# A hybrid decoder layer in fp32: Strassen products without the short step in one more chunk, and a tile of its own for the rows that scale x

## The chip, the cores and the metric

One core of one Trainium2 chip runs the whole layer. The metric is the device time of one execution in microseconds, the median of several runs. The profile is of one further execution of the same program.

## The reference, cut to what matters

256 tokens of width 2048, one layer, all in fp32. Between the parts stands a layer norm with gain g and offset b.

```
x <- LN0(alpha*x + 0.5*SwiGLU_1(x))
z  = x @ W_in                      (nine projections)
m  = sigmoid(gate_conv)*(yA @ Wa) + sigmoid(gate_hgrn)*(yB @ Wb)
x <- LN1(alpha*x + m @ W_out)
x <- LN2(alpha*x + 0.5*SwiGLU_2(x))
x <- LN3(alpha*x + sigmoid(x @ W_pg) * (p @ W_pp))

def swiglu(x, w_in, w_out):
    a, u = jnp.split(x @ w_in, 2, axis=-1)
    return (jax.nn.silu(a) * u) @ w_out
```

The hidden width of each SwiGLU is 5504, so w_in is 2048 x 11008 and w_out 5504 x 2048.

## The kernel before, in words

**Products.** The tokens are two tiles of 128 (t = 0, 1). Activations stand still in TensorE, weights stream past it, 512 columns at a time. For fp32 accuracy each product of a k-tile (128 rows of weights) is three passes (`passes`, L1035): high half of x with high half of the weights (L1039), high with low (L1040), low with high (L1041). The high half of a weight tile (`wh`) is a cast by ScalarE (L973), the low half (`wl`) a subtraction by VectorE (L984); raw weights come by DMA from the SP queue (L913) into a ring `raw` of 4 tiles of two k-tiles each, 512 KB. The operands of x are made the same way by `halves`: `xh` by ScalarE (L284), `xl` by VectorE (L285).

**Stages.** lead1, ffn1, tail1, hgrn, merge, lead2, ffn2, tail2, ple. A feed-forward stage cuts its hidden width into 11 chunks: ch 0 with 512 columns and ch 1 with 384 are plain products (`Unit`); ch 2 to 10 are `Quad`s, which do the two tiles of tokens and two halves of the k-tiles by Strassen's seven products for eight. ch 0 runs in the lead stage, the rest in ffn. Between chunks stand the products with w_out (`out_unit`) for the chunks before; these go in groups of two chunks and four columns of 512, two columns after each chunk. So two of them follow ch 2 and ch 3 each, of 7 k-tiles, and two follow ch 4 and ch 5 each, of 8.

**Short step.** A Quad multiplies 16 k-tiles: 8 in two full Strassen steps, and 8 that are left. With the argument `short` (L79) two of those 8 are multiplied by one more Strassen step of half the size (`short_step`: h1 to h4, with three additions of weights by VectorE at L952, called h2, h3 and h4; h2 is 1024 columns wide, the others 512), in the order `ORDER`; without it all 8 are plain products, in the order `ORDER8`. `ORDER8` has 60 products of a k-tile, `ORDER` 59. In before ch 2 is without the short step and ch 3 to 10 with it (L498).

**The end of a chunk.** When the seven banks of a Quad are done, five small functions combine them on VectorE (all recorded at L463) and ScalarE: `first` to `fifth`. `third` begins with `silu<-h,bank`, which needs the bank of product p6.

**Norms.** `layer_norm(t, i, scale, stat)` scales x by mean and deviation (L425), and makes the operands of the next stage with g and b folded in by ScalarE (L419). x itself, for the residual, still has to be multiplied by g and added to b: that is `affine_rows`, for each column of 512 and both tiles of tokens, deferred to a later tick (a tick is one step of some matmuls). It loads a row of g and a row of b, spread over 128 partitions (256 KB each), into a slot of the weights' ring (tile `gb`, L397), and four ticks later multiplies (L402) and adds (L403). For layer norm 1, the one ahead of lead2, column c's rows are loaded 10 + 7c ticks after the norm.

**Sums.** For the Strassen products the operands need sums of x's quarters (`sums`, called at ch 1, additions at L319) in the tiles `yT` and in one more tile `s` from the ring "11" of region `high`.

**What sets the order.** Each engine runs its instructions in the order in which a scheduler put them. `feed` issues loads, additions, casts and splits of weights as slots come free; `defer` and `tick` place the rest. A queue never passes an instruction that waits.

Of the kernel before, what the change touches and what calls it, by code (L numbers as in the profile page):

```python
# [10 lines left out]
F32 = mybir.dt.float32  # L11
# [6 lines left out]
P = 128  # L18
D = 2048
S = 256  # L20
NT = 2
DFF = 5504
CW = 1024
CC = 512
KG = 2
NRAW = 4
# [110 lines left out]
def hybrid_layer(ctx: ExitStack, tc: tile.TileContext, x, p, ln_g, ln_b, ffn1_w_in, ffn1_w_out, mix_w_in,  # L137
# [13 lines left out]
    rp = pool("rp", side="right")  # L151
    st = pool("st", side="right")
    region = {}
# [8 lines left out]
    def open_region(kind):  # L162


        if kind.startswith("tail"):
            region.pop("hctx").close()
        region["pool"] = reopen("ctx", kind, "left")
        region["kind"] = kind
        if kind.startswith("lead"):
            region["high"] = reopen("hctx", kind + "h", "right")  # L170
            held.update(dict.fromkeys(HIGH, 0), on=False)
        if kind.startswith("ffn"):
            roles = {"a": 7, "t": 1}
        else:
            roles = {"t": 2, "a": 4, "h": 2}
        free = deque(sorted(banks, key=lambda n: used_at[n]))
        for role, n in roles.items():
            role_of[role] = [free.popleft() for _ in range(n)]
# [22 lines left out]
    def defer(delay, fn):  # L201
        insort(later, (state["tick"] + delay, fn), key=lambda e: e[0])
# [37 lines left out]
    def settle(c):  # L240

        while c in unsettled:
            later.pop(0)[1]()
# [61 lines left out]
    plain = {}  # L305

    def high(part, name):

        return region["high"].tile([P, KG, CC], F32, tag="b" + part, name=name, bufs=HIGH[part])
# [5 lines left out]
        return plain[t, c // 2][:, c % 2, :]  # L315

    def sums(stat):
        def both(o, a, b, op):
            nc.vector.tensor_tensor(out=o, in0=a, in1=b, op=op)  # L319

        def four(x11, x12, x21, x22, s1, s2, s3, s4):
            both(s3, x11, x21, ALU.subtract)
            both(s1, x21, x22, ALU.subtract)
            both(s2, s1, x11, ALU.subtract)
            both(s4, x12, s2, ALU.add)

        lo, hi, spare = [plain[t, 0] for t in range(NT)], [plain[t, 1] for t in range(NT)], high("11", "s")
        x = [lo[0][:, 0, :], lo[0][:, 1, :], lo[1][:, 0, :], lo[1][:, 1, :]]
        s3 = spare[:, 0, :]

        def low_sums():
            four(*x, x[2], x[0], s3, x[1])

        def made(n, src):
            halves(stat, n, 0, src, 4, "s")


        short = spare[:, 1, :]

        def short_sums():  # L340
            y = [hi[t][:, 0, i * P : (i + 1) * P] for t in range(NT) for i in range(2)]
            four(*y, *(short[:, i * P : (i + 1) * P] for i in range(4)))

        def made_short():
            halves(stat, "short", 0, short, 4, "s")
            h, l = stat.parts["short", 0]
            for i in range(4):
                stat.parts[f"s{i + 1}", 1] = h[:, i : i + 1, :], l[:, i : i + 1, :]

        def delta(c):  # L350
            d = hi[0][:, c % 2, :]
            both(d, d, hi[1][:, c % 2, :], ALU.subtract)
            halves(stat, "d", c, d, 4, "s")

        todo = (low_sums, lambda: made("s1", x[2]), lambda: made("s2", x[0]), lambda: made("s3", s3),
                lambda: made("s4", x[1]), short_sums, made_short, lambda: delta(2), lambda: delta(3),
                lambda: held.update(on=True))
        for i, fn in enumerate(todo):
            defer(1 + 2 * i, fn)
# [30 lines left out]
        nc.vector.bn_aggr(mv, stats[t])  # L390
        return mv[:, 0:1], rsqrt_of(mv[:, 1:2], 1, 1.0, LN_EPS / scale ** 2)

    def affine_rows(i, c, ts):

        gb = rp.tile([P, KG, CC], F32, tag="raw", name="gb", bufs=NRAW)
        for a, src in enumerate((ln_g, ln_b)):
            nc.sync.dma_start(gb[:, a, :], src[0, i : i + 1, c * CC : (c + 1) * CC].broadcast_to([P, CC]))  # L397

        def apply():
            for t in ts:  # L400
                xc = xt[t][:, c * CC : (c + 1) * CC]
                nc.vector.tensor_tensor(out=xc, in0=xc, in1=gb[:, 0, :], op=ALU.mult)  # L402
                nc.vector.tensor_tensor(out=xc, in0=xc, in1=gb[:, 1, :], op=ALU.add)  # L403
            unsettled.remove(c)

        defer(4, apply)

    def layer_norm(t, i, scale, stat):

# [19 lines left out]
        if t == NT - 1:  # L429
            for c in range(4):  # L430
                unsettled.add(c)
                defer(10 + 7 * c if stat is x2 else 40 + 20 * c, lambda c=c: affine_rows(i, c, range(NT)))

    def layer_norm_out(t, gb):
        mean, r = moments(t, 1.0)
# [7 lines left out]
    units = []  # L443

    def ffn(name, xs, w_in, w_out, ln_i, nxt):
# [7 lines left out]
        def in_units(ch, g, ci):  # L453
            c0 = starts[ch]
            w = starts[ch + 1] - c0
            if ch > 1:
# [32 lines left out]
                def fifth(ps):  # L489
# [5 lines left out]

                after = deque([(("p1",), first), (("p3", "p5"), second), (("p6", "p7"), third),
                               (("p2",), fourth), (("p4",), fifth)])
                units.append(Quad(xs, w_in, (c0, DFF + c0), CC, after, ch > 2))  # L498
                return
            silu = {}  # L500

# [45 lines left out]
    x0, x1, x2, x3 = Stat(), Stat(), Stat(), Stat()  # L547
# [322 lines left out]
    for u in units:  # L870
# [17 lines left out]
        for blk in u.blocks:  # L888
            for ks in blk:
                i = len(plan)  # L890
# [118 lines left out]


    open_region(units[0][0])

    warm = ptile("a", "warm")
# [112 lines left out]
```

## Time and profile before

| | us |
|---|---|
| median of 3 runs | 2228.91 |
| lowest, highest | 2226.73, 2230.83 |
| profiled execution | 2225.66 |
| its span | 2223.9 |

The granted TensorE clock has a mean of 0.996 in that execution. Line numbers in the profile are those of the kernel before. PE is TensorE's matmuls, PEld its weight loads, DVE is VectorE, ACT is ScalarE, SP the queue that issues most DMAs. A matmul of 512 columns is shown as 0.39 us long, but successive ones overlap: the pace is read from their starts. In brackets behind a row of a timeline stands how long the engine was idle ahead of it and what ended that.

### The profile page before, as it was taken

How to read it: one execution, taken by the hardware profiler on the slowest of the kernel's cores; microseconds unless marked ns; L12 is line 12 of the kernel's file. 1: busy time of each engine (PE TensorE's matmuls, PEld its weight loads, DVE VectorE, ACT ScalarE, POOL GpSimd, SP SyncE). 2: the span in 40 equal slices, each digit the busy share in tenths (PEclk: the TensorE clock that was granted, in tenths of full speed). 3: DMA queues.
4: the chain of work that ended last, by engine and by line, in shares of the span. 5: the costliest groups of instructions: out<-in, count | busy, mean ns of one | idle time of the engine just before them, and what ended most of it. 6: DMA issues, size and time to landing. Idle time of an engine off the chain costs nothing.

```text
span 2223.9 us, 27084 instructions
## 1 busy us (share of the span) xinstructions
PE 2193.5 (99%) x10062; PEld 1827.2 (82%) x10062; DVE 1755.3 (79%) x2042; ACT 1156.0 (52%) x1357; POOL 9.9 (0%) x32
## 2 busy tenths in 40 slices
PE   9999999999999999999999999999999999999997
PEld 7987888888887888888888888788788888888886
DVE  6788999999985678567555875769899999999668
ACT  5555555555565434444444443645556555556463
POOL 1000000000000000000000000000000000000000
PEclk9999999999999999999999999999999999999998
DMA  7656666666663665555565665576566666665564
GB/s 252 222 185 198 210 205 189 191 207 208 199 202 113 203 193 171 181 161 152 189 194 184 206 193 191 181 231 189 182 199 206 201 211 198 202 202 188 173 216 156
DMA packets 225848, 430.00 MB, mean 193 GB/s; under 512 B 14252, under 2 KB 22964, under 8 KB 225716
## 3 DMA queue, kind: packets, MB, share of 16 engines
q1 hardware_dynamic: 225716, 428.27, 60.9%
q8 instruction: 79, 1.29, 0.2%
q14 instruction: 53, 0.43, 0.1%
HBM read 426.12 MB, written 2.10 MB: 193 GB/s over the span
## 4 chain that ended last, share of the span: by engine, by line
PE 92%; DVE 4%; DMA 2%; issue 1%; ACT 1%; SPq 0%; DVEq 0%; ACTq 0%
PE bank L1040 30%; PE bank L1041 30%; PE bank L1039 30%; PE bank L274 2%; DVE wl L984 2%; PE bank L636 1%; DMA gb<-in_ln_g_dram 1%; DVE raw L952 1%; ACT wh L973 0%; DMA gb<-in_ln_b_dram 0%; DMA raw<-in_ffn_w_in_dram 0%; DMA x<-in_x_dram 0%; DVE x L438 0%; DVE x L439 0%; ACT y L419 0%
## 5 line engine op out<-in xcount | busy, mean ns | idle before, releaser
L973 ACT CAST wh<-raw 128x1024 fp32r<-128x1024 f32 (+2 forms) x944 | 960.0, 1032 | 833.9 <-PE bank L1041 519.2
L984 DVE TENSOR_TENSOR wl<-raw,wh 128x1024 fp32r<-128x1024 f32 (+2 forms) x944 | 1113.6, 1200 | 283.1 <-ACT wh L973 262.0
L1040 PE MATMUL bank<-wl,xh 128*128 128x512 f32 (+1 forms) x1688 | 652.1, 387 | 1.2 <-DVE wl L984 1.0
L1041 PE MATMUL bank<-wh,xl 128*128 128x512 f32 (+1 forms) x1688 | 651.3, 387 | 1.5 <-DVE xl L285 1.5
L1039 PE MATMUL bank<-wh,xh 128*128 128x512 f32 (+1 forms) x1688 | 648.2, 388 | 1.7 <-ACT xh L284 1.6
L1039 PEld LDWEIGHTS bank<-wh,xh 128*128 128x128 f32 x1688 | 317.9, 188 | 62.9 <-ACT xh L284 2.6
L1040 PEld LDWEIGHTS bank<-wl,xh 128*128 128x128 f32 x1688 | 317.9, 188 | 62.7 <-DVE wl L984 2.8
L1041 PEld LDWEIGHTS bank<-wh,xl 128*128 128x128 f32 x1688 | 317.5, 188 | 62.6 <-DVE xl L285 2.2
L1040 PE MATMUL bank<-wl,gh 128*128 128x512 f32 x896 | 349.9, 391 | 4.3 <-DVE wl L984 4.1
L1041 PE MATMUL bank<-wh,gl 128*128 128x512 f32 x896 | 349.8, 392 | 0.0
L1039 PE MATMUL bank<-wh,gh 128*128 128x512 f32 x896 | 348.5, 393 | 0.0
L952 DVE TENSOR_TENSOR raw<-raw,raw 128x1024 f32<-128x1024 f32 (+1 forms) x176 | 206.3, 1172 | 6.2 <-DMA raw<-in_ffn_w_in_dram 4.5
L1040 PEld LDWEIGHTS bank<-wl,gh 128*128 128x128 f32 x896 | 168.7, 188 | 40.6 <-DVE wl L984 6.0
L1041 PEld LDWEIGHTS bank<-wh,gl 128*128 128x128 f32 x896 | 168.5, 188 | 34.5
L1039 PEld LDWEIGHTS bank<-wh,gh 128*128 128x128 f32 x896 | 168.3, 188 | 34.4 <-ACT pp L841 0.2
L1040 PE MATMUL bank<-wl,sh 128*128 128x512 f32 x464 | 180.6, 389 | 0.0
L1041 PE MATMUL bank<-wh,sl 128*128 128x512 f32 x464 | 180.5, 389 | 0.0
L1039 PE MATMUL bank<-wh,sh 128*128 128x512 f32 x464 | 179.2, 390 | 0.0
L1041 PEld LDWEIGHTS bank<-wh,sl 128*128 128x128 f32 x464 | 87.1, 188 | 18.2
L1039 PEld LDWEIGHTS bank<-wh,sh 128*128 128x128 f32 x464 | 87.1, 188 | 18.0
L1040 PEld LDWEIGHTS bank<-wl,sh 128*128 128x128 f32 x464 | 87.1, 188 | 18.0
L526 DVE TENSOR_TENSOR x<-x,bank 128x512 f32<-128x512 f32 x64 | 43.6, 681 | 21.6 <-PE bank L1041 21.5
(173 smaller groups left out, 1005.1 us busy)
## 6 DMA issues: line engine op xcount, KB each, us to landing
raw<-in_ffn_w_in_dram SPq DMA_DIRECT2D x288, 512.0 KB, 4.5
raw<-in_mix_w_in_dram SPq DMA_DIRECT2D x176, 512.0 KB, 4.7
raw<-in_ffn_w_out_dram SPq DMA_DIRECT2D x168, 512.0 KB, 4.7
raw<-in_ffn_w_in_dram SPq DMA_DIRECT2D x64, 256.0 KB, 3.0
raw<-in_mix_w_out_dram SPq DMA_DIRECT2D x32, 512.0 KB, 5.2
raw<-in_ple_w_gate_dram SPq DMA_DIRECT2D x32, 512.0 KB, 5.5
raw<-in_ffn_w_in_dram SPq DMA_DIRECT2D x32, 384.0 KB, 4.0
raw<-in_branch_w_conv_dram SPq DMA_DIRECT2D x16, 512.0 KB, 4.7
```

Source lines behind the costliest of these rows:

```text
L274: state["turned"] = nc.tensor.transpose(tp[:, i * P : (i + 1) * P], src[:, i * P : (i + 1) * P], ident).ins
L526: nc.vector.tensor_tensor(out=xc, in0=xc, in1=acc, op=ALU.add)
L636: nc.tensor.matmul(gp[:, (h * 2 + t) * 64 : (h * 2 + t + 1) * 64], kd[:, h, t * P : (t + 1) * P], qd[:, h, t, :], start=True, stop=True)
L952: nc.vector.tensor_tensor(out=out, in0=a, in1=b, op=ALU.add)
L973: nc.scalar.copy(h[:, :n, :w], raw[:, :n, :w])
L984: nc.vector.tensor_tensor(out=l[:, :n, :w], in0=raw[:, :n, :w], in1=h[:, :n, :w].bitcast(F32), op=ALU.subtract)
L1039: nc.tensor.matmul(acc, sh, wh[:, a, :n], start=first, stop=False)
L1040: nc.tensor.matmul(acc, sh, wl[:, a, :n], start=False, stop=False)
L1041: nc.tensor.matmul(acc, sl, wh[:, a, :n], start=False, stop=last)
```

## The change

It has two parts. First, `ch > 2` becomes `ch > 3`: ch 3 of both feed-forward stages is done without the short step, as ch 2 was. Second, the tile that `sums` used as `s` is now taken when a lead stage opens, under the name `spare`; in lead2 the rows of g and b for all four columns go by way of this one tile, and not by the weights' ring. Column c's rows are loaded 2 + 8c ticks after the norm and applied six ticks later. `sums` first finishes what is still to be scaled (`settle`). Layer norms 0 and 2 keep the ring and their ticks.

```diff
@@ open_region
             held.update(dict.fromkeys(HIGH, 0), on=False)
+            region["spare"] = high("11", "spare")
@@ sums
     def sums(stat):
+        for c in range(4):
+            settle(c)
+
@@ sums
-        lo, hi, spare = [plain[t, 0] for t in range(NT)], [plain[t, 1] for t in range(NT)], high("11", "s")
+        lo, hi, spare = [plain[t, 0] for t in range(NT)], [plain[t, 1] for t in range(NT)], region["spare"]
@@ affine_rows
-    def affine_rows(i, c, ts):
-
-        gb = rp.tile([P, KG, CC], F32, tag="raw", name="gb", bufs=NRAW)
+    def affine_rows(i, c, ts, gb, delay):
+
+        if gb is None:
+            gb = rp.tile([P, KG, CC], F32, tag="raw", name="gb", bufs=NRAW)
@@ affine_rows
-        defer(4, apply)
+        defer(delay, apply)
@@ layer_norm
-                defer(10 + 7 * c if stat is x2 else 40 + 20 * c, lambda c=c: affine_rows(i, c, range(NT)))
+                if stat is x2:
+                    defer(2 + 8 * c, lambda c=c: affine_rows(i, c, range(NT), region["spare"], 6))
+                else:
+                    defer(40 + 20 * c, lambda c=c: affine_rows(i, c, range(NT), None, 4))
@@ in_units
-                units.append(Quad(xs, w_in, (c0, DFF + c0), CC, after, ch > 2))
+                units.append(Quad(xs, w_in, (c0, DFF + c0), CC, after, ch > 3))
```

In the changed kernel the lines are a few further down: splits of weights are L992, additions of weights L960, steps at a chunk's end L471, the scaling L407 and L408, the loads of its rows L402, weights' DMAs L921, `xl` L286.

**VectorE at the end of ch 3 in before** (first feed-forward stage; `silu` and `h` are the tiles of the chunk's end, the addition of `raw_1838` is h2 of ch 4):

```order
L984 TENSOR_TENSOR wl<-raw_1539,wh 128x1024
L463 TENSOR_TENSOR silu<-silu,bank_83 128x512
L952 TENSOR_TENSOR raw_1362<-raw_1362,raw_1539 128x1024
L463 TENSOR_TENSOR silu<-h,bank_79 128x512
L984 TENSOR_TENSOR wl<-raw_1362,wh 128x1024
L463 TENSOR_TENSOR silu<-silu 128x512
L463 TENSOR_TENSOR h<-h,bank_81 128x512
L952 TENSOR_TENSOR raw_1838<-raw_1551,raw_1658 128x1024
L984 TENSOR_TENSOR wl<-raw,wh 128x1024 x2
```

**VectorE at the end of ch 4 in after** (the addition of `raw_2318` is h2 of ch 5):

```order
L992 TENSOR_TENSOR wl<-raw_2016,wh 128x1024
L471 TENSOR_TENSOR silu<-silu,bank_85 128x512
L960 TENSOR_TENSOR raw_1839<-raw_1839,raw_2016 128x1024
L471 TENSOR_TENSOR silu<-h,bank_82 128x512
L992 TENSOR_TENSOR wl<-raw_1839,wh 128x1024
L471 TENSOR_TENSOR silu<-silu 128x512
L471 TENSOR_TENSOR h<-h,bank_83 128x512
L960 TENSOR_TENSOR raw_2318<-raw_2028,raw_2135 128x1024
L992 TENSOR_TENSOR wl<-raw,wh 128x1024 x2
```

The same kinds of instructions stand in the same order, one chunk later; in after the end of ch 3 reads as that of ch 2 in before, with the addition for the next chunk ahead of `silu<-h,bank`.

**VectorE at the start of lead2 in before** (`x1_95` is the second tile of tokens, `mv`, `w` and `m` are its norm, `xl_11131` the first low operand of x2):

```order
L984 TENSOR_TENSOR wl_11013<-raw_10900,wh_11012 128x1024
L984 TENSOR_TENSOR wl_11077<-raw_10938,wh_11076 128x1024
L984 TENSOR_TENSOR wl_11083<-raw_10950,wh_11082 128x1024
L825 SCALAR_TENSOR_TENSOR x1_95<-x1_95,bank1_80 128x512
L984 TENSOR_TENSOR wl_11074<-raw_10912,wh_11073 128x1024
L367 BN_STATS bn_10618<-x1_95 128x6
L390 BN_AGGR mv_11050<-bn_10618 128x2
L375 TENSOR_SCALAR w_11052<-mv_11050 128x1
L377 TENSOR_SCALAR m_11053<-mv_11050 128x1
L984 TENSOR_TENSOR wl_11089<-raw_11016,wh_11088 128x1024
L285 TENSOR_TENSOR xl_11131<-yT_11121,xh_11130 128x512
```

**The same place in after** (`xl_11121` is the first low operand):

```order
L992 TENSOR_TENSOR wl_11058<-raw_10889,wh_11057 128x1024
L394 BN_AGGR mv_11033<-bn_10607 128x2
L992 TENSOR_TENSOR wl_11073<-raw_10939,wh_11072 128x1024
L379 TENSOR_SCALAR w_11035<-mv_11033 128x1
L381 TENSOR_SCALAR m_11036<-mv_11033 128x1
L407 TENSOR_TENSOR x0_94<-x0_94,spare_11056 128x512
L408 TENSOR_TENSOR x0_94<-x0_94,spare_11056 128x512
L992 TENSOR_TENSOR wl_11079<-raw_11064,wh_11078 128x1024
L992 TENSOR_TENSOR wl_11085<-raw_11070,wh_11084 128x1024
L286 TENSOR_TENSOR xl_11121<-yT_11111,xh_11120 128x512
```

Scaling of column 0 of the first tile of tokens and a split more now stand right ahead of the first low operand.

**SP's queue in lead2 in before** (`gb` are slots of the weights' ring):

```order
L913 DMA raw_11279<-in_ffn2_w_in_dram 128x2x512
L913 DMA raw_11291<-in_ffn2_w_in_dram 128x2x512
L397 DMA gb_11293<-in_ln_g_dram 128x512
L397 DMA gb_11293<-in_ln_b_dram 128x512
L913 DMA raw_11306<-in_ffn2_w_in_dram 128x2x384
L913 DMA raw_11318<-in_ffn2_w_in_dram 128x2x384
L913 DMA raw_11330<-in_ffn2_w_in_dram 128x2x384
L913 DMA raw_11360<-in_ffn2_w_in_dram 128x2x384
L397 DMA gb_11370<-in_ln_g_dram 128x512
L397 DMA gb_11370<-in_ln_b_dram 128x512
L913 DMA raw_11411<-in_ffn2_w_in_dram 128x2x384
```

**SP's queue in lead2 in after**, columns 1 to 3:

```order
L921 DMA raw_11109<-in_ffn2_w_in_dram 128x2x512
L402 DMA spare_11056<-in_ln_g_dram 128x512
L402 DMA spare_11056<-in_ln_b_dram 128x512
L402 DMA spare_11056<-in_ln_g_dram 128x512
L402 DMA spare_11056<-in_ln_b_dram 128x512
L402 DMA spare_11056<-in_ln_g_dram 128x512
L402 DMA spare_11056<-in_ln_b_dram 128x512
L921 DMA raw_11259<-in_ffn2_w_in_dram 128x2x512
```

The rows of g and b that had weights between them now follow one another, each into the same tile. On VectorE this stretch reads in after:

```order
L407 TENSOR_TENSOR x0_94<-x0_94,spare_11056 128x512
L407 TENSOR_TENSOR x1_95<-x1_95,spare_11056 128x512
L286 TENSOR_TENSOR xl_11191<-yT_11181,xh_11190 128x512
L408 TENSOR_TENSOR x0_94<-x0_94,spare_11056 128x512
L286 TENSOR_TENSOR xl_11209<-yT_11181,xh_11208 128x512
L408 TENSOR_TENSOR x1_95<-x1_95,spare_11056 128x512
L407 TENSOR_TENSOR x0_94<-x0_94,spare_11056 128x512
L407 TENSOR_TENSOR x1_95<-x1_95,spare_11056 128x512
L408 TENSOR_TENSOR x0_94<-x0_94,spare_11056 128x512
L408 TENSOR_TENSOR x1_95<-x1_95,spare_11056 128x512
L323 TENSOR_TENSOR yT_11150<-yT_11150,yT_11218 128x512
L286 TENSOR_TENSOR xl_11228<-yT_11218,xh_11227 128x512
```

Between the scalings of columns 1 and 2 (L407 multiplies, L408 adds) and the low operands there is no split of weights any more.

## Rows read from the trace of the kernel before

**Rows 1.** The page's busy time of each engine (share of the span, number of instructions), and the shares of the chain that ended last, by engine.
```profile
PE 2193.5 (99%) x10062; PEld 1827.2 (82%) x10062; DVE 1755.3 (79%) x2042; ACT 1156.0 (52%) x1357; POOL 9.9 (0%) x32
...
PE 92%; DVE 4%; DMA 2%; issue 1%; ACT 1%; SPq 0%; DVEq 0%; ACTq 0%
```

**Rows 2.** TensorE's waits over the whole span: which instruction, what it waited for: us in total, how often, the longest.
```profile
PE bank L1040 <- DVE wl L984: 5.1, 4, 2.0
...
PE bank L1039 <- ACT xh L284: 1.6, 2, 0.8
...
PE bank L1041 <- DVE xl L285: 1.5, 2, 0.8
PE bank L274 <- ACT pp L841: 1.5, 1, 1.5
PE bank L274 <- DVE gl L285: 1.0, 1, 1.0
```

**Rows 3.** TensorE's timeline at the end of ch 3 in the first feed-forward stage (two rows) and in the second: start, us, engine and line, operation, and in brackets the idle time ahead of it and what ended it.
```profile
192.50 0.40 PE L1041 MATMUL bank<-wh,xl 128*128 128x512 f32 x1
194.94 0.53 PE L1040 MATMUL bank<-wl,gh 128*128 128x512 f32 x1 [2.04 <-DVE wl L984]
...
1599.92 0.39 PE L1041 MATMUL bank<-wh,xl 128*128 128x512 f32 x1
1602.36 0.50 PE L1040 MATMUL bank<-wl,gh 128*128 128x512 f32 x1 [2.05 <-DVE wl L984]
```

**Rows 4.** TensorE's timeline around the change from the merge stage to lead2: the first and the last of 24 matmuls, the first two matmuls on x2's operands that waited, and the first use of a low operand of the third column of the second half.
```profile
1401.64 0.39 PE L1039 MATMUL bank<-wh,mh 128*128 128x512 f32 x1
...
1406.86 0.39 PE L1041 MATMUL bank<-wh,ml 128*128 128x512 f32 x1
...
1412.19 0.50 PE L1039 MATMUL bank<-wh,xh 128*128 128x512 f32 x1 [0.79 <-ACT xh L284]
...
1413.72 0.72 PE L1041 MATMUL bank<-wh,xl 128*128 128x512 f32 x1 [0.80 <-DVE xl L285]
...
1436.11 0.39 PE L1041 MATMUL bank<-wh,xl 128*128 128x512 f32 x1
```

**Rows 5.** Groups of VectorE's instructions by line and shape, from 145 to 190 us (chunks 2 and 3 of the first feed-forward stage): count, busy us, mean ns of one, idle us ahead of them.
```profile
L984 DVE TENSOR_TENSOR wl<-raw,wh 128x1024 fp32r<-128x1024 f32 x22 | 25.9, 1221 | 2.3 <-ACT wh L973 2.3
L952 DVE TENSOR_TENSOR raw<-raw,raw 128x1024 f32<-128x1024 f32 x8 | 9.8, 1221 | 0.1
...
L952 DVE TENSOR_TENSOR raw<-raw 128x512 f32<-128x512 f32 x1 | 0.7, 684 | 0.0
```

**Rows 6.** VectorE's timeline at the end of ch 3 of the first feed-forward stage.
```profile
189.59 0.69 DVE L463 TENSOR_TENSOR silu<-h,bank 128x512 f32<-128x512 f32 x1 [2.61 <-PE bank L1041]
190.19 1.22 DVE L984 TENSOR_TENSOR wl<-raw,wh 128x1024 fp32r<-128x1024 f32 x1
...
191.93 0.68 DVE L463 TENSOR_TENSOR h<-h,bank 128x512 f32<-128x512 f32 x1
192.53 1.22 DVE L952 TENSOR_TENSOR raw<-raw,raw 128x1024 f32<-128x1024 f32 x1
193.67 2.35 DVE L984 TENSOR_TENSOR wl<-raw,wh 128x1024 fp32r<-128x1024 f32 x2
```

**Rows 7.** Three stretches: length, busy time (and instructions) of PE, PEld, DVE, ACT and POOL, the granted TensorE clock as a share of full speed, the share of the DMA engines, GB/s.
```profile
195.20:198.70 3.50, 3.50 (x10) 2.71 (x10) 3.50 (x5) 0.00 (x0) 0.00 (x0) 0.51 0.65 221
1413.80:1417.30 3.50, 3.50 (x9) 2.76 (x10) 3.01 (x7) 3.50 (x10) 0.00 (x0) 0.51 0.86 281
1600.00:1610.00 10.00, 7.95 (x35) 6.30 (x34) 9.48 (x12) 2.73 (x3) 0.00 (x0) 1.00 0.77 236
```

**Rows 8.** VectorE's timeline at the start of lead2.
```profile
1405.57 3.49 DVE L984 TENSOR_TENSOR wl<-raw,wh 128x1024 fp32r<-128x1024 f32 x3
...
1412.99 0.68 DVE L285 TENSOR_TENSOR xl<-yT,xh 128x512 fp32r<-128x512 f32 x1
```

**Rows 9.** ScalarE's timeline at the same place.
```profile
1411.48 0.66 ACT L284 CAST xh<-yT 128x512 fp32r<-128x512 f32 x1
1412.78 1.05 ACT L973 CAST wh<-raw 128x1024 fp32r<-128x1024 f32 x1 [0.64 <-DMA raw<-in_ffn_w_in_dram]
```

**Rows 10.** The SP queue's timeline from 1406.5 to 1409 us: weights for lead2 (start, us until the last is issued, count).
```profile
1406.85 1.47 SPq L913 DMA_DIRECT2D raw<-in_ffn_w_in_dram  x2
```

**Rows 11.** Pieces of the chain of waits from 1430 to 1480 us that are landings of rows of g and b: start, us, what.
```profile
1437.09 5.95 DMA gb<-in_ln_g_dram
...
1447.60 5.80 DMA gb<-in_ln_g_dram
...
1456.82 3.75 DMA gb<-in_ln_g_dram
...
1470.06 6.71 DMA gb<-in_ln_b_dram
```

**Rows 12.** All rows of g and b in the trace (tile gb): us from issue to landing.
```profile
DMA to landing us min/median/max: 3.6/5.6/7.2
```

**Rows 13.** TensorE's timeline in the 384-wide chunk of the second feed-forward stage and at the start of ple.
```profile
1470.30 0.66 PE L274 MATMUL bank<-ident,h 128*128 128x128 f32 x4 [0.98 <-DVE gl L285]
...
1480.35 0.44 PE L1040 MATMUL bank<-wl,xh 128*128 128x384 f32 x1 [0.55 <-DVE wl L984]
...
2118.42 0.63 PE L274 MATMUL bank<-ident,x 128*128 128x128 f32 x4 [1.46 <-ACT pp L841]
```

## The prediction

> **What bounds the kernel now.** First the page's busy table and its chain. TensorE is busy for 99% of the span, and 92% of the chain that ended last is its own work; VectorE is busy for 79% [rows 1]. So an instruction that VectorE or ScalarE is spared is worth something only where TensorE waits for that engine. Second, TensorE's waits: a dozen in 2223.9 us. The largest sum is for a low half of a weight (wl) from VectorE, 5.1 us in four waits; the others this change can reach are for xh, for xl, for gl and for pp [rows 2]. Third, where they are. Two of about 2.04 us stand at the end of the second Strassen chunk (ch 3), one in each feed-forward stage [rows 3]. Most of the others lie at the starts of stages that follow a norm, lead2 among them, where x2 is made and scaled. The change touches the ends of chunks and lead2, so I cost each by itself.
>
> **Part 1, the second chunk without the short step.** *Matmuls.* The short step does an odd pair of k-tiles with 7 products for 8; the long order spends one k-tile product more, and each product is three passes. Per stage 180 matmuls take the place of 177, so 6 more in all. TensorE's pace in an undisturbed stretch: 24 starts from 1401.64 to 1406.86 are 23 steps in 5.22 us, 0.227 us each [rows 4]. 6 x 0.227 = **+1.4 us**, on the path, since TensorE is the path.
>
> *What VectorE and ScalarE are spared.* Per stage 7 k-tiles of short and plain weights become 4, which is 1.5 casts and 1.5 splits of two k-tiles fewer, and three additions go (1024, 512 and 512 columns): by the groups 1.5 x 1.22 + 1.22 + 0.68 + 0.68 = 4.4 us of VectorE [rows 5]. Off the path it is worth nothing. It would be worth something in the 2.04 us wait.
>
> *Where that wait goes.* VectorE's timeline shows its cause: VectorE reaches the third step of the chunk's end (silu from h and a bank), stands 2.61 us until TensorE has finished the bank, and then has a split, two more steps and an addition of 1024 columns (the short step's first sum for the next chunk) ahead of the split that TensorE wants: 189.59 to 193.67 and the first of two splits, done about 194.9 [rows 6], when TensorE starts again [rows 3]. It is an order of rows, not a lack of VectorE time, and the order says where it goes. In after, the end of ch 3 reads as the end of ch 2 did, with the next chunk's addition ahead of the third step, and there before has no wait of this kind. But the end of ch 4 now reads, row for row, as the end of ch 3 did: addition, third step, split, two steps, addition for the first short chunk, splits. Each chunk's banks are done at the same place of its order, so I take the same wait there: **0** net per stage. Bounds: if it doesn't come back, -2.04 and -2.05; if it grows by one split, +1.2 each. I take 0, as 10 or more rows on both sides agree. With the first of these waits goes a stretch at half the granted clock (0.51, that is 1.2 GHz, for 3.5 us from 195.2), while after the other the clock stayed up [rows 3, 7]. The stretch costs about half its length, 1.7 us; I leave it in, and it goes if the wait goes.
>
> **Part 2, g and b of layer norm 1 by way of one spare tile.** The rows move from ticks 10, 17, 24, 31 after the norm to 2, 10, 18, 26, and the additions for the Strassen operands now wait until all four columns are scaled. Three things follow.
>
> *The first rows at lead2's start.* In after, VectorE's queue has the scaling of column 0 of x0 (L407, L408) and two splits ahead of xl_11121, the first low operand that TensorE needs. In before only one split is ahead: xl starts at 1412.99 and TensorE's L1041 at 1413.72 [rows 4, 8]. When does VectorE get to L407? Its rows from 1405.57 on hold one split fewer before the addition of x1, and one more after it, so about 1412.1. When are the rows of g there? SP issues two weights from 1406.85 on, in 1.47 us [rows 10], then g: about 1408.5. Landings of these 256 KB rows took 3.75 us in one place and 5.8 to 6.71 in three, among weights [rows 11]; two 512 KB weights are in flight, so I take 4.3: g at about 1412.9, b at about 1413.6. L407 and L408 (0.69 each) then end about 1414.3, the two splits 1416.6, xl 1417.2. Against 1413.72: **+3.5 us**. Lower bound: with the rows in time it is ScalarE that is later, since it now casts two weights ahead of xh where there was one, and the second can't start before 1412.78, when its weight has landed [rows 9]: cast done 1413.8, its split 1415.0, xl 1415.7, so +2.0. Upper bound: landings of 5.9 give +5. Of the half-clock stretch that stands here already (1413.8 to 1417.3) [rows 7] I take the same cost.
>
> *Columns 1 to 3.* One tile serves all columns, so g of the next column is issued only when both scalings by the last g are done, and b when both additions are; and no split is queued between. From 1417.2 VectorE has x1's norm, three splits, two operands and x1's column 0 to do, some 8.5 us: column 1 is issued about 1425.7 and lands, among weights, about 1430.7, in time for the operand behind it. Its second addition stands behind two operands and ends about 1434.5; b of column 2 is issued then and lands 3.9 us later, 1438.4. Two additions by it, one sum and then xl_11228: 1440.8. TensorE takes this operand first at 1436.11 in before [rows 4], so 3.5 us later and one matmul more in after, 1439.8: **+1.0 us**. Bounds: 0 if a landing takes 2.9 us, +4.3 if those of columns 2 and 3 take 5.9. I take the short landings, as SP has no weight between these rows and the ring is full.
>
> *What goes.* In before these rows are waited for amid the 384-wide chunk, and TensorE loses 0.98 us at 1470.30 for gl, 0.55 at 1480.35 for wl and some tenths more, with the refill of its queue [rows 13]. In after the scalings are over by then: **-1.6 us** (0 to -2.0). Cover: these splits now run ahead; if the additions, now in one piece behind column 3, crowd the same place, it is 0.
>
> **Small shifts.** The number of slots used has changed, so casts and operands meet a little differently at the first products behind the other norms. The order at the start of hgrn has xh and xl one place later, +0.3 (between 0 and 0.8, the waits there now [rows 2]); at ple the 1.46 us wait for pp [rows 13] mostly goes, -0.7 (from -1.5 to +1).
>
> **Sum.** +1.4 + 0 + 3.5 + 1.0 - 1.6 + 0.3 - 0.7 = **+3.9 us**. The profiled execution took 2225.66 (span 2223.9), 3.25 below the median of the runs, 2228.91; it becomes 2229.6, and the median **2232.8**. A measurement of this kernel can tell about 0.2% from no change, 4.5 us: 2224.4 to 2233.4 counts as the same, and my forecast lies near its upper edge.
>
> **A rule against the rows.** The 4.3 and 3.9 us above are taken from landings of such rows in the trace, 3.6 to 7.2 us over all of them [rows 12]. The Trainium skill, page "DMA: Bandwidth & Descriptors", section "Anatomy of one DMA", fits a DMA of its path as 2.0 us and the bytes over 436 GB/s: an estimate of 2.6 us for 256 KB; no landing here was that short. By that figure of the Trainium skill the rows of g would be there when VectorE arrives and column 3 would be in time: rival C below.
>
> **The rivals.**
> *B, the one tile serialises, slower.* Every column's rows are issued only behind the last column's use, among a burst of weights; the landings are like those at 1437.09 and 1470.06, about 5.9 us and more, not 3.75 [rows 11]. Then lead2's start costs +5, columns 2 and 3 +4.3, and only 0.5 of the later waits goes: 1.4 + 5 + 4.3 - 0.5 - 0.4 = +9.8, **2238.7**. It decides from landings of about 5 us. For it: three of four landings in lead2 were that long. Against it: SP has nothing between the rows of columns 1 to 3. The Trainium skill, page "Trainium Kernel Development and Optimization", section "Best Practices", asks for two buffers so that a DMA overlaps with work; the one spare tile is the opposite, and by it B would be the likelier.
> *C, the rows are hidden.* All rows land in time, only the order of casts costs: 1.4 + 2.0 - 2.0 - 0.4 = +1.0, **2229.9**. For it: g's issue lies 3.6 us before its use, and the shortest landing here was 3.6. Against it: the median landing is 5.6 [rows 12].
> *D, the wait of ch 3 is gone for good.* VectorE, spared 4.4 us per stage, is ahead when ch 4 ends, and the two waits and the half-clock stretch go: the forecast without -2 x 2.05 - 1.7, and with C's or a better start of lead2: 3.9 - 5.8 - 1.2 = -3.1, **2225.8**. For it: the first wait of 2.61 us shows VectorE was early, so time was not short. The same speaks against it: more of VectorE's time doesn't help where it waits for a bank in a fixed order.
>
> **How the numbers follow.** Forecast 0.42 (its own span about 2230 to 2236), B 0.28, C 0.18, D 0.12. The forecast's cases split at 2233.4: some 0.25 of the 0.42 below it and 0.17 above. Slower by over 0.2%: 0.17 and B's 0.28, 0.45. Within: 0.25, C's 0.18 and half of D, 0.49. Faster by over 0.2%: half of D, 0.06, since only a D with more gain than I can name passes 2224.4. The range takes in B's centre and D's upper half: 2226.5 to 2239.0, which leaves out about 0.06 below and 0.12 above.
>
> **What would show it.** Right: 10068 matmuls in the busy table; in both stages no wait at the end of ch 3 and one of about 2 us at the end of ch 4; at lead2's start a wait of L1041 for xl that ends about 3.5 us later than now, with VectorE idle for about 0.8 us for the spare tile's DMA; one more wait for xl some 25 us later; none of the waits at 1470 and 1480. Wrong: no wait at the end of ch 4 (D), idle time of VectorE for the spare tile of 3 us and more per column (B), or none at all (C).

## The result, and the profile after

The changed kernel takes 2236.31 us (median of 9 runs, 2232.44 to 2238.59), the kernel before 2227.77 on the same chips (9 runs, 2225.47 to 2230.83). The ratio is 1.0036, interval [1.0027, 1.0044]: 8.0 us slower. The profiled execution took 2238.59 us, 12.9 more than that of before; it lies 2.3 above its median and that of before 2.1 below its own, so some 4 of the 12.9 belong to these two executions and not to the change. A second profile of the changed kernel (e12) took 2236.65. One execution of e5 (2759.69 us) and one of e9 (3164.09 us) had a mean granted clock of only 0.750 and 0.653; they count in the medians below and not in the ratios.

Where the difference arises can be read off the starts of TensorE's transposes, which stand at the same places of both programs (timeline of TensorE, us; a group has up to eight transposes, and the same one of a group is taken in both; the last row is the last matmul):

| place | before | after | difference | arose in this stretch |
|---|---|---|---|---|
| h of ch 0 | 56.14 | 57.01 | +0.9 | start of lead1 |
| x, end of ffn1 | 701.07 | 702.46 | +1.4 | +0.5 |
| x, second tile, in hgrn | 710.82 | 715.84 | +5.0 | **+3.6** |
| x, in lead2 | 1407.09 | 1412.14 | +5.05 | 0.0 |
| x, second tile, in lead2 | 1420.45 | 1432.92 | +12.5 | **+7.4** |
| h of ch 1 | 1497.49 | 1506.87 | +9.4 | **-3.1** |
| end of ffn2 | 1997.85 | 2009.05 | +11.2 | +1.8 |
| x, at ple | 2106.86 | 2119.73 | +12.9 | +1.7 |
| last matmul | 2209.96 | 2223.01 | +13.05 | +0.2 |

First TensorE's waits of the changed kernel, which answer to [rows 2] (us in total, times, longest):

```profile
PE bank L1049 <- DVE xl L286: 6.2, 2, 5.0
PE bank L1048 <- DVE wl L992: 4.1, 2, 2.0
PE bank L1047 <- ACT xh L285: 2.9, 1, 2.9
PE bank L275 <- ACT y L424: 2.5, 2, 2.2
```

Two waits for wl are left, the two long ones; those of [rows 13] in the 384-wide chunk are gone. One wait for xl grew from 0.8 to 5.0 us, one for xh from 0.8 to 2.9, and one for y, which was 0.7 us in before, is 2.2. The +0.9 at the start of lead1 comes with a wait of 0.67 us for a cast of a weight at 26.67; e12, the same kernel, has no such wait and +0.25 there, so it belongs to the execution.

The end of ch 4 in the changed kernel, TensorE in both feed-forward stages, which answers to [rows 3]:

```profile
254.20 0.39 PE L1049 MATMUL bank<-wh,xl 128*128 128x512 f32 x1
256.64 0.80 PE L1048 MATMUL bank<-wl,gh 128*128 128x512 f32 x1 [2.05 <-DVE wl L992]
...
1670.13 0.39 PE L1049 MATMUL bank<-wh,xl 128*128 128x512 f32 x1
1672.56 0.67 PE L1048 MATMUL bank<-wl,gh 128*128 128x512 f32 x1 [2.05 <-DVE wl L992]
```

And VectorE there, which answers to [rows 6]:

```profile
251.29 0.69 DVE L471 TENSOR_TENSOR silu<-h,bank 128x512 f32<-128x512 f32 x1 [2.61 <-PE bank L1049]
251.89 1.22 DVE L992 TENSOR_TENSOR wl<-raw,wh 128x1024 fp32r<-128x1024 f32 x1
...
254.23 1.22 DVE L960 TENSOR_TENSOR raw<-raw,raw 128x1024 f32<-128x1024 f32 x1
255.36 2.36 DVE L992 TENSOR_TENSOR wl<-raw,wh 128x1024 fp32r<-128x1024 f32 x2
```

It is the same wait, to a hundredth, one chunk later: 2.61 us for the bank, then the same five instructions.

The start of hgrn, TensorE, first in before:

```profile
701.07 1.03 PE L274 MATMUL bank<-ident,x 128*128 128x128 f32 x8
702.93 0.50 PE L1039 MATMUL bank<-wh,xh 128*128 128x512 f32 x1 [0.82 <-ACT xh L284]
...
704.33 0.66 PE L274 MATMUL bank<-ident,x 128*128 128x128 f32 x4 [0.67 <-ACT y L419]
705.68 0.50 PE L1041 MATMUL bank<-wh,xl 128*128 128x512 f32 x1 [0.69 <-DVE xl L285]
```

and in the changed kernel:

```profile
702.46 1.03 PE L275 MATMUL bank<-ident,x 128*128 128x128 f32 x8
705.71 0.66 PE L275 MATMUL bank<-ident,x 128*128 128x128 f32 x4 [2.22 <-ACT y L424]
706.22 0.51 PE L1047 MATMUL bank<-wh,xh 128*128 128x512 f32 x1
...
708.19 0.80 PE L1049 MATMUL bank<-wh,xl 128*128 128x512 f32 x1 [1.18 <-DVE xl L286]
```

A third group of transposes, which needs a bank that ScalarE is still reading (it waits for y), stands ahead of the first matmul; in before it stood behind the first two. TensorE idles 3.4 us in two pieces (2.2 in three in before), and what follows runs at half the clock, 0.50, that is 1.2 GHz (windows, changed kernel, among them the two places at the end of ch 4; the third number from the right is the granted clock):

```profile
256.00:260.00 4.00, 3.36 (x9) 2.70 (x10) 4.00 (x5) 0.00 (x0) 0.00 (x0) 0.57 0.49 166
708.00:712.00 4.00, 3.81 (x9) 3.04 (x10) 3.44 (x10) 3.77 (x10) 0.00 (x0) 0.50 0.60 227
1672.00:1678.00 6.00, 5.44 (x17) 4.35 (x18) 6.00 (x8) 0.00 (x0) 0.00 (x0) 0.72 0.65 219
```

The clock falls behind both waits of 2.05 us this time, where in before it fell behind the first alone [rows 7]. That is not a property of the kernel: e12 runs the same program, and there it falls behind the second wait alone.

The start of lead2 in the changed kernel, TensorE, which answers to [rows 4]:

```profile
1419.30 0.80 PE L1047 MATMUL bank<-wh,xh 128*128 128x512 f32 x1 [2.85 <-ACT xh L285]
...
1425.55 0.80 PE L1049 MATMUL bank<-wh,xl 128*128 128x512 f32 x1 [5.03 <-DVE xl L286]
```

VectorE there, which answers to [rows 8]:

```profile
1420.32 0.69 DVE L407 TENSOR_TENSOR x<-x,spare 128x512 f32<-128x512 f32 x1 [3.53 <-DMA spare<-in_ln_g_dram]
1421.92 0.69 DVE L408 TENSOR_TENSOR x<-x,spare 128x512 f32<-128x512 f32 x1 [0.91 <-DMA spare<-in_ln_b_dram]
1422.53 2.35 DVE L992 TENSOR_TENSOR wl<-raw,wh 128x1024 fp32r<-128x1024 f32 x2
1424.80 0.69 DVE L286 TENSOR_TENSOR xl<-yT,xh 128x512 fp32r<-128x512 f32 x1
```

and the DMA issues from 1405 to 1425 us there (count, KB, median us to landing):

```profile
raw<-in_ffn_w_in_dram SPq DMA_DIRECT2D x6, 512.0 KB, 4.6
spare<-in_ln_g_dram SPq DMA_DIRECT2D x1, 256.0 KB, 6.8
spare<-in_ln_b_dram SPq DMA_DIRECT2D x1, 256.0 KB, 7.9
```

VectorE stands still for 4.4 us with two splits and the operand behind it, and the first rows land later than any row of g in [rows 11].

### The profile page after: what moved, and what is told of

It is laid out like the page before. It is cut to its first block, busy times and chain, and to the rows that moved or that the text cites. A ratio compares the mean times of both kernels' runs of the same rounds, so it can differ in the third digit from the quotient of the medians.

```text
span 2236.8 us, 27060 instructions
## 1 busy us (share of the span) xinstructions
PE 2199.8 (98%) x10068; PEld 1833.0 (82%) x10068; DVE 1747.9 (78%) x2032; ACT 1154.6 (52%) x1353; POOL 10.4 (0%) x32
## 4 chain that ended last, share of the span: by engine, by line
PE 93%; DVE 3%; DMA 2%; ACT 1%; issue 1%; SPq 0%; DVEq 0%; ACTq 0%
PE bank L1049 30%; PE bank L1048 30%; PE bank L1047 30%; PE bank L275 1%; DVE wl L992 1%; PE bank L644 1%; DMA raw<-in_ffn_w_out_dram 1%; ACT wh L981 1%; DMA raw<-in_ffn_w_in_dram 0%; DMA spare<-in_ln_b_dram 0%; DMA raw<-in_ple_w_gate_dram 0%; DVE x L446 0%; DVE x L447 0%; DVE raw L960 0%; DVE xl L286 0%
## 5 line engine op out<-in xcount | busy, mean ns | idle before, releaser
L992 DVE TENSOR_TENSOR wl<-raw,wh 128x1024 fp32r<-128x1024 f32 (+2 forms) x940 | 1109.6, 1200 | 296.9 <-ACT wh L981 275.3
L960 DVE TENSOR_TENSOR raw<-raw,raw 128x1024 f32<-128x1024 f32 (+1 forms) x172 | 202.5, 1177 | 5.7 <-DMA raw<-in_ffn_w_in_dram 4.2
```

Of the source, the lines that this page charges most:

```text
L960: nc.vector.tensor_tensor(out=out, in0=a, in1=b, op=ALU.add)
L992: nc.vector.tensor_tensor(out=l[:, :n, :w], in0=raw[:, :n, :w], in1=h[:, :n, :w].bitcast(F32), op=ALU.subtract)
```

## The experiments

All but e12 are medians of 5 to 11 runs, and the ratio is to the kernel before on the same chip, with its 95% interval in brackets. Not all experiments ran on one chip; kernels from different chips are compared by their ratios. What a stretch costs is read off the starts of transposes in the one profiled execution, as in the table above.

**e1: the chunk alone.**

```diff
-                units.append(Quad(xs, w_in, (c0, DFF + c0), CC, after, ch > 2))
+                units.append(Quad(xs, w_in, (c0, DFF + c0), CC, after, ch > 3))
```

> Kernel before with the one edit ch > 3, the rows of g and b in the weights' ring as before. Theory (the loss has two places, and one of them comes with the chunk): 6 matmuls +1.4 us; the start of hgrn has the casts of the changed kernel ahead of its first operands, +3.6; the start of lead2 has one split and one cast more ahead of the first low operand, +2.0; the waits around 1470 to 1485 us stay; the 2.04 us waits stand at the end of ch 4. Sum +7, about 2235. Rival (the rows' tile carries the loss, the chunk only its matmuls): +1.4, about 2229, and hgrn starts as in the kernel before.

2234.45 us, ratio 1.0030 [1.0019, 1.0041]. In its profile hgrn's start costs 3.8 and lead2's start 1.8 us by the same transposes, and the two waits of 2.04 us stand at the end of ch 4. The theory holds: most of the loss comes with the half of the change that looks like six matmuls, because it shifts what stands ahead of the first operands of later stages.

**e2: the rows' tile alone** (the changed kernel with `ch > 2`).

> Changed kernel with ch > 2, so only the tile for the rows of g and b is left. Theory: hgrn starts as in before; at lead2 the first scaling stands ahead of the first low operand and waits for a landing of about 6.8 us, so this operand is some 4 us later than in before; the waits at 1470 to 1485 us go, -3.1. Sum about +1, 2229. Rival (the rows' tile carries the loss): +6.6, about 2234.5.

2228.87 us, 1.0006 [0.9997, 1.0015]: no difference that can be told. hgrn starts as in before. At lead2 the scaling waits 2.92 us for g, TensorE 4.3 for xl, and the 384-wide chunk gives 3.1 back. By the ratios the two parts add up, 1.0030 and 1.0006 against 1.0036, to within their intervals. At lead2's start they don't: 1.8 us in e1 and 3.3 in e2, but 7.4 together. The order shows a reason: in e2 the first low operand stands between the scaling's multiplication and its addition, so it waits for g alone, and in the changed kernel it stands behind both and two splits.

**e3 and e4: the first scaling out of the operand's way.** Both put the scaling of column 0 behind the low operand of the second column on VectorE; e3 is the changed kernel with it, e4 has `ch > 2` as well.

```diff
-        nc.vector.tensor_tensor(out=lf, in0=src, in1=hf.bitcast(F32), op=ALU.subtract)
+        state["xl", t, g] = nc.vector.tensor_tensor(out=lf, in0=src, in1=hf.bitcast(F32), op=ALU.subtract).ins
...
+                with tc.issue_after(state["xl", 0, 1]) if gb is region.get("spare") and c == 0 else nullcontext():
```

> Changed kernel, the scaling of column 0 put behind the low operand of the second column on VectorE; the rows' loads stay where they are. Theory (VectorE standing still for the landing of g and b ahead of the operand costs about 5 us at lead2's start, the order of casts the other 2): the wait for xl falls from 5.0 to about 1 us, the whole from +8.5 to about +3.5 over before, 2231. Rival (the operand would be late anyway, since ScalarE's casts and the weights' landings hold it): less than 2 us gained, 2234.5 and more.

> Both: ch > 2, and the scaling of column 0 behind the low operand of the second column. Lead2 then starts with the order of before. Theory: only the gain of the rows' own tile is left, the waits at 1470 to 1485 us: -3 us, about 2225, faster than both kernels. Rival (one tile for four columns serialises and costs elsewhere, for instance at the third column's operand or at the sums): 0 to +3, 2228 to 2231.

e3: 2230.62 us, 1.0012 [1.0003, 1.0021], 5.3 us under the changed kernel by the ratios. e4: 2224.45 us, 0.9987 [0.9978, 0.9995], faster than both kernels, though by little. In e3 the rows of g and b land after 7.3 and 8.2 us, as late as in the changed kernel, and nothing waits for them; lead2's start costs 1.7 us and not 7.4. So most of the price at lead2 was the place of the scaling in VectorE's queue, and the rows' own tile is worth 3.1 us in the chunk behind (the 384-wide one, in both profiles).

**e10: the rows first.** The same scaling ahead of the operand, but its rows are loaded when lead2 opens, and SP issues lead2's weights behind them.

```diff
-    units.append(("lead2", lambda: None))
+    units.append(("lead2", lambda: affine_rows(1, 0, range(NT), region["spare"], 8)))
...
+        with tc.issue_after(state["rows"]) if "rows" in state and region["kind"] == "lead2" else nullcontext():
             nc.sync.dma_start(raw[:, at : at + n, :width], src)
```

> The changed kernel; the rows of g and b for column 0 are loaded when lead2 opens, and SP issues lead2's weights behind them, where they stood behind two weights. On VectorE the scaling still stands ahead of the first low operand. Theory (the landings of 6.8 and 7.9 us are long because two weights of 512 KB and more are in flight with them): they come down to about 4 us, VectorE waits 1 us or less, the first low operand is some 6 us earlier, 2230 to 2231. Rival (a landing at this place takes 6.8 us whatever is in flight): VectorE still waits over 2 us, and less than 3 us are gained, 2233.5 and more.

2229.42 us, 1.0012 [1.0003, 1.0021]. VectorE at lead2's start in e10:

```profile
1415.20 0.69 DVE L409 TENSOR_TENSOR x<-x,spare 128x512 f32<-128x512 f32 x1 [0.76 <-DMA spare<-in_ln_g_dram]
...
1417.39 0.69 DVE L410 TENSOR_TENSOR x<-x,spare 128x512 f32<-128x512 f32 x1 [0.24 <-DMA spare<-in_ln_b_dram]
1418.00 0.68 DVE L286 TENSOR_TENSOR xl<-yT,xh 128x512 fp32r<-128x512 f32 x1
```

g lands 3.9 us after its issue where it took 6.8, and b, by the end of VectorE's wait for it, about 5.7 after where it took 7.9. Same size, same queue, and issued only 1 us earlier in the stage: with the pair of weights ahead of them g took 2.9 us more and b some 2.2. The gain of e10 isn't the landing alone: with the rows first, one split less stands ahead of the low operand, and no cast of a weight ahead of the first xh.

**e5: hgrn's start.** On top of e3, ScalarE's y of column 1 is put behind the cast of xh of column 0 there.

```diff
+                with tc.issue_after(state["xh", t, c - 1]) if stat is x1 and t == 0 and c == 1 else nullcontext():
                     nc.scalar.activation(y[:, a * P : (a + 1) * P], tp[:, a * P : (a + 1) * P], AF.Identity,
```

> The kernel of e3_scale_behind_xl, and at hgrn's start ScalarE's four pieces of y for column 1 put behind the cast of xh of column 0; TensorE's third group of transposes then stands behind its first two matmuls again, as in before. Theory (the 3.6 to 3.8 us at hgrn's start come from this order: TensorE stands in a transpose that waits for a bank, and then runs at the low clock): they go to about +0.3, the whole is 3.4 us under e3, 2227.2. Rival (the casts of weights ahead of xh hold it): less than 1 us gained, 2230.

2230.46 us, 1.0013 [1.0004, 1.0022], as e3: the rival's time came. TensorE's transposes stand as in before, and yet it idles 3.0 us in all where before has 2.2, and the clock falls again. TensorE in e5:

```profile
703.14 0.50 PE L1049 MATMUL bank<-wh,xh 128*128 128x512 f32 x1 [1.33 <-ACT xh L285]
...
704.55 0.66 PE L275 MATMUL bank<-ident,x 128*128 128x128 f32 x4 [0.68 <-ACT y L426]
...
706.21 0.80 PE L1051 MATMUL bank<-wh,xl 128*128 128x512 f32 x1 [1.00 <-DVE w L379]
```

and in e8, below:

```profile
702.25 0.50 PE L1050 MATMUL bank<-wh,xh 128*128 128x512 f32 x1 [1.33 <-ACT xh L285]
...
703.66 0.66 PE L275 MATMUL bank<-ident,x 128*128 128x128 f32 x4 [0.68 <-ACT y L426]
704.61 0.50 PE L1052 MATMUL bank<-wh,xl 128*128 128x512 f32 x1 [0.29 <-DVE w L379]
```

The rival's reason carries some 0.5 us of it: on ScalarE the first y stands behind a cast of a weight, where in before it starts as soon as its bank is ready, and the wait for xh is 1.33 us where before has 0.82. But e8 has the same wait for xh, its 2.3 us of idle time in the same three places were not followed by a fall of the clock, and the stretch cost 0.1. What of the 3.6 in the changed kernel is idle time and what clock can be read: 3.4 - 2.2 = 1.2 us more idle time, the other 2.4 us at half the clock. So at this place the order of transposes was not the only cause, and the larger part of the price is the clock.

**e6, e9 and e11: does the wait at a chunk's end follow the first short chunk?** e6 is e3 with `ch > 4`, e9 the kernel before with `ch > 4`, e11 is e6 with `ch > 5`.

> The kernel of e3_scale_behind_xl with ch > 4: ch 4 too is without the short step, 12 matmuls more than in before (+2.7 us). By VectorE's order the end of ch 5, now the first short chunk, reads as in the changed kernel, where it has no wait. Theory (the wait of 2.04 us belongs to one order of rows at the end of a chunk and not to the first short chunk as such): no such wait in either feed-forward stage, -4.1 us and -1.7 us for a stretch at the low clock; with hgrn's start +3.6 and the later waits -2.3 it comes to about 2226. Rival (the wait moves on to ch 5): 2232.

> The kernel before with the one edit ch > 4; rows of g and b in the weights' ring. Theory (e6's gain is mostly that of the chunks: no wait of 2 us at any chunk's end, no stretch at the low clock behind one, a shorter idle time at hgrn's start; the rows' own tile adds 2.3 us): 2218.5. Rival (the gain needs both halves): 2224 and more.

> The kernel of e6_ch4 with ch > 5, 6 matmuls more again. Theory (once no chunk's end has the wait, one more chunk without the short step costs its matmuls alone): +1.4 over e6, 2217.5. Rival (VectorE, spared another 9 us, is worth something on the path): 2216 or less.

e6: 2216.10 us, 0.9952 [0.9939, 0.9964]. e9: 2218.28 us, 0.9959 [0.9945, 0.9972]. e11: 2218.95 us, 0.9965 [0.9952, 0.9977]. All of TensorE's waits in e6:

```profile
PE bank L275 <- ACT yT L425: 2.4, 3, 1.2
PE bank L1024 <- POOL ident masks.py:199: 1.6, 1, 1.6
PE bank L275 <- ACT y L425: 1.3, 1, 1.3
PE bank L275 <- DMA x<-in_x_dram: 1.0, 1, 1.0
PE bank L1048 <- ACT xh L285: 0.9, 1, 0.9
PE bank L1050 <- DVE xl L286: 0.2, 1, 0.2
```

No wait for wl is left, and up to the last matmul the clock falls at lead2's start only. So the wait belongs to an order of rows, not to the first short chunk: in the kernel before, one more chunk without the short step loses 6.6 us (e1) and two more gain 8.8 (e9). e6 came out 10 us better than I expected; its profile shows where most of it lies: at hgrn's start it idles 1.3 us instead of 3.4 (-1.0 against before where I had +3.6), lead2's start has no extra split (+0.7 and not +1.8), and at ple the wait for pp is gone (-1.7). Each is a place where an order came out well; I did not foresee them. e9 shows that the gain is mostly that of the chunks. By the ratios it lies 1.6 us over e6, within the intervals; in the profiles e9 has a wait of 2.20 us for a cast of a weight in the 384-wide chunk, with a stretch at the low clock behind it (0.57), and e6, with the rows' own tile, has none. e11 lies 2.9 over e6 by the ratios, where its six matmuls are 1.4, so neither the theory nor the rival was right; its intervals overlap with e6's, and in its profile the rest stands at ple, which has no such gain of 1.7.

**e7 and e8: the wait by itself.** The step that waits for p6's bank is put behind the latest split, in e7 on top of e4, in e8 on top of e5.

```diff
-                    both(e, made["c11"], ps["p6"], ALU.add)
+                    with tc.issue_after(state["wl"]):
+                        both(e, made["c11"], ps["p6"], ALU.add)
```

> The kernel of e4_rows_behind_xl (ch > 2), and at each chunk's end the step that waits for the bank of p6 put behind the latest split on VectorE, so that the addition for the next chunk and the splits are done while the bank is not ready. Theory (VectorE stands still there with ready work behind it): the two waits of 2.04 us go, -4 to -6 us with the clock, 2219 to 2220.5. Rival (the splits aren't ready there, or the later step holds up TensorE's next bank): no gain or a loss, 2224 and more.

> The changed kernel with all three orders: e5_y_behind_xh and the step of e7_third_behind_wl. What is left of the change against e7 is 6 matmuls (+1.4) and the order of casts at lead2's start (+1.8). Theory: 3.2 us over e7, 2222 to 2223.5. Rival (a chunk without the short step costs or saves something else): off by over 2 us.

e7: 2225.81 us, 0.9991 [0.9982, 1.0000], no gain over e4. e8: 2225.78 us, 0.9995 [0.9986, 1.0004]. In e7 the wait of 2.04 us at the end of ch 3 is gone in both stages, and one of 0.75 us stands at the end of ch 4 of the second. But at the end of the last chunk TensorE now waits, where e4, which differs by this edit alone, has no wait. TensorE in e7, both stages:

```profile
637.97 0.73 PE L1049 MATMUL bank<-wh,gh 128*128 128x512 f32 x2 [1.20 <-ACT wh L983]
...
2038.21 0.50 PE L1050 MATMUL bank<-wl,gh 128*128 128x512 f32 x1 [2.67 <-DVE wl L994]
```

So VectorE does stand there with ready work behind it, as the theory has it, and in the second stage the gain is given back at the last chunk, where the splits are the ones that come late (ffn1 -1.8 us, ffn2 +1.4 against before). e8 against e5 gains 4.7 us, and it ends where e7 does instead of 3.2 us above, so that estimate of what is left of the change failed: here, too, the ends of the two stages and hgrn's start came out differently, and I can't separate them.

**e12: the changed kernel again.**

> The changed kernel once more, for a second profile of it. The first is 12.9 us longer than that of the kernel before, the medians differ by 8.5. Theory (the orders are fixed, landings and the clock are not): the same waits at hgrn's start (2.2 and 1.2 us), the 2.05 us at the end of ch 4 twice, and no wait at 1470 to 1485 us; what differs is the length of the first landings at lead2 (5 to 8 us) and which of the waits is followed by a stretch at the low clock. Rival (the places themselves change): waits at other places.

2236.65 us, one run. hgrn's start +3.7, lead2's start +7.5, the 384-wide chunk -3.1, all as in the first profile; the scaling waits 3.23 and 1.24 us for g and b, and the waits of 2.05 us stand at the end of ch 4 in both stages (256.01 and 1670.68). What differs is ffn1 (-0.9 against +0.5) and the first microseconds. Most of the difference in ffn1 is the clock, which stayed up behind the first of these waits and fell behind the second (windows of e12):

```profile
256.00:258.00 2.00, 1.99 (x9) 1.64 (x10) 2.00 (x3) 0.00 (x0) 0.00 (x0) 1.00 0.40 101
...
1672.00:1674.00 2.00, 2.00 (x6) 1.61 (x5) 2.00 (x3) 0.00 (x0) 0.00 (x0) 0.50 0.79 272
```

The places are fixed; whether a wait is followed by a stretch at the low clock is not.

## Why the prediction was right or wrong

The time lies in the range, at 2236.3 against a forecast of 2232.8, and the sign of the sum was right; but "within 0.2%" had the larger chance, and the measured ratio lies beyond it. That the range held is in part luck: the terms for lead2's start, the later waits and hgrn's start all lie outside the bounds that I gave them, and they partly cancel; my own span for the forecast ended at about 2236, and the range reaches 2239.0 only because it takes in B's centre, though the second half of B didn't come. By its steps:

- **The six matmuls**: right, 10068 in the busy table, 1.4 us.
- **The wait that moves from ch 3 to ch 4**: right in mechanism, place and size, 2.05 us in both stages; the reading of VectorE's order row for row carried. What it said of the clock (left as it is) was off by one stretch in these profiles: it fell behind the second stage's wait too, and in e12 behind that one alone. D is refuted for this change, and e6 shows what D's gain is when the order does come out otherwise.
- **lead2's start**: the mechanism was right (the scaling and one more split ahead of the first low operand, one more cast ahead of xh), the size was not: 3.5 forecast with an upper bound of 5, 7.4 measured. The step that failed is the landing: I took 4.3 us, nearest to the short row of [rows 11], where 6.8 and 7.9 came. xl ended at 1425.5, that is 1420.4 on the clock of before, against my 1417.2; b's landing, 3.2 us later than I had it, is all of that; the other 0.6 is the clock. e1 gives the part of the casts and splits, 1.8 (my lower bound: 2.0), e10 the landing, e3 the place in the queue. The row that lay nearest in kind was one among weights, and I chose the one with little beside it.
- **Columns 1 to 3**: 1.0 forecast, 0 measured. The landings were 4.6 us in column 1 and 3.0 to 3.2 in columns 2 and 3, and TensorE itself came 7.4 us later: the operand ended at 1448.4 and was used at 1448.6. My sign of B, VectorE idle 3 us and more per column for the tile, came for column 0 (4.4 us) and column 1 (3.95), not for column 2 (1.95) and column 3 (none), and from column 1 on TensorE didn't wait for it. This half of B didn't come, so B's sum was as wrong as mine; its first half, long landings at lead2's start, did.
- **The later waits that go**: -1.6 forecast, -3.1 measured, beyond my bound of -2.0. The waits that are gone are 0.98, 0.55 and 0.41 us, 1.9 in all; I allowed little for the time that TensorE needs behind each of them to fill its queue again, which by this difference is 1.2 us.
- **Small shifts**: the step that failed outright. +0.3 at hgrn's start, at most 0.8, was read off one place in ScalarE's and VectorE's order; on TensorE's own row a third group of transposes had moved ahead of the first matmul, and that, with a cast of a weight more on ScalarE and the half clock behind it, cost 3.6. At ple -0.7 was forecast, +0.2 came; the stretch ahead of it, where I expected nothing, cost 1.7, about half of it a wait of 0.73 us at 2075.82 for gh, the high half of hidden values that ScalarE casts, and the refill behind it, the rest not settled.
- **Sum**: 3.9 forecast. The stretches of the profiled execution give 13.05, the ratio 8.0. The two profiles of the changed kernel differ by 1.9 us, of which 1.4 lie in ffn1, where the clock fell in the one and not in the other; hgrn, lead2 and the 384-wide chunk are the same in both. What else makes a median execution shorter they don't tell.

The Trainium skill, page "DMA: Bandwidth & Descriptors", section "Anatomy of one DMA", gives its fit, by which 256 KB are an estimate of 2.6 us, for DMAs on its SWDGE (gpsimd) path; these rows are issued by SP, so it wasn't made for them. They don't bear it out: the shortest took 3.0 us in the changed kernel, the first 6.8. C, in which all rows land in time, fell with the first landing. The rule of two buffers (the Trainium skill, page "Trainium Kernel Development and Optimization", section "Best Practices") is not what decided either: columns 1 to 3, which share the one tile, made VectorE wait 5.9 us in the changed kernel and cost TensorE nothing, and with the first scaling out of the way (e4) the one tile gains.

The best kernel of the study is e6, 2216.1 us: two more chunks without the short step in each stage, the rows by way of their own tile, and the first scaling behind the operand.

## What to carry to other kernels

An edit of a few instructions can move the waits of stages far behind it, since it shifts what stands ahead of each stage's first operands (here 6 matmuls cost 6.6 us, e1): read the order of every engine there, TensorE's own rows first, before calling a shift small. Where an instruction that waits for a DMA has ready work behind it on its engine, price the landing by rows that had the same traffic issued ahead of them, or move the instruction; when a wait moves from one place to the next, try one place more, since it may not come back.

## What the runs showed of the hardware that I had not expected

- A load of 256 KB on the SP queue landed 6.8 to 8.2 us after its issue behind two weights of 512 KB (changed kernel, e3) and 3.9 to about 5.7 us when issued ahead of them (e10).
- The same wait of 2.04 to 2.05 us of TensorE was followed by a stretch at half the clock in some places and executions and by none in others: in before at 195 us (0.51) and not at 1602 (1.00), in the changed kernel at both places in one profile (0.57 and 0.72 in windows wider than the stretch) and at the second alone in the other (1.00 at 256 us in e12). A wait of fixed length has no fixed price.
